# Column units of a hybrid decoder layer: all products with the high weights first, then all with the low weights

## The chip, the cores and the metric

The kernel runs on one core of one Trainium2 chip. The metric is the device time of one execution in microseconds, the median of several runs. Lower is better.

## The reference

One decoder layer on 256 tokens of width 1024 in float32. A modulated RMS norm gives `h`; one input projection gives ten blocks of 1024 columns; a causal attention with 8 heads and a short convolution run side by side; each has a SiLU gate and an output projection; the two are merged through sigmoid gates and go through a last projection and a residual, then a final RMS norm. With 256 tokens there is one attention block, so attention is plain causal attention with a relative bias.

```python
mod = jax.nn.silu(c) @ w_ada + b_ada
shift, scale, gate = jnp.split(mod, 3, axis=-1)
h = rmsnorm(x, norm_g) * (1 + scale[:, None, :]) + shift[:, None, :]
q, k, v, g_attn, cb, cc, cx, g_conv, m_attn, m_conv = jnp.split(h @ w_in, IN_OFFSETS, axis=-1)
attn = moba_attention(split_heads(q), split_heads(k), split_heads(v), rel_bias)
y_attn = (attn.transpose(0, 2, 1, 3).reshape(bsz, seq, ATTN_WIDTH) * jax.nn.silu(g_attn)) @ w_o_attn
y_conv = (short_conv(cb, cc, cx, conv_w) * jax.nn.silu(g_conv)) @ w_o_conv
merged = jax.nn.sigmoid(m_attn) * y_attn + jax.nn.sigmoid(m_conv) * y_conv
x = x + gate[:, None, :] * (merged @ w_out)
return rmsnorm(x, final_g)
```

## The kernel before

Precision is kept by splitting each float32 operand into a high part, held in the type `float32r`, and a low part, the rest. A product is then high times high, high times low and low times high, all summed in one PSUM bank.

The stages follow one another on PE (TensorE). After a start-up, the slab stage (L196 to L208) makes q and k for all heads, eight row tiles of the weights one after the other. Then come the V products (`rows_mm`, L349), and then 36 **column units** (`unit`, L332): four each of cc, cx, cb, gc, ga, ma, mc on the moving operand `H`, and four each of oa and oc, in turns, on `GA` and `GC`. The attention of the heads is put between the first units by a table of slots: scores (`pS`), transposes of the softmax (`pT`) and outputs (`pO`). At the end the output projection (`rows_mm` again, tiles `ao`) and the residual follow.

One unit makes 256 output columns as two halves (`t`) of 128. Its moving operand has, for each of the eight row tiles `k`, 512 columns: 256 of the high part, then 256 of the low part. For each `k` and half there are two products. The one with the high weights (L340) takes all 512 columns and fills a whole bank: the first 256 columns high times high, the others high times low. The one with the low weights (L341) takes the first 256 columns and adds to the bank's second half. `fold` (L324) then adds the two halves of the bank: ACT (ScalarE) copies the second half to SBUF (L326), DVE (VectorE) adds the first (L327). Below, the product of L340 is called wide, that of L341 narrow.

A unit's weights come as one DMA of 1 MB on SP's queue into one of five `raw` buffers. `split` (L67) makes the high part on ACT (L73) and the low part on DVE (L74), both for the whole unit at once, into one of three `hi` and three `lo` buffers. PSUM has eight banks, which all products share in turns (`bank`, L56).

The Tile framework finds the dependencies, puts in the semaphores, and plans at build time the order of the instructions on every engine, by priority in program order and by what its own model of durations finds ready. What is wrapped in `pin` keeps the order of the program; the products of a unit, its split and its fold are not pinned. Each engine then works through its own list in order.

Of the kernel before, what the change touches and what calls it, by code (L numbers as in the profile page):

```python
# [17 lines left out]
P = 128  # L18
D = 1024
S = 256  # L20
NH = 8
KT = D // P
# [21 lines left out]
def layer_kernel(ctx: ExitStack, tc, x, c, vec, wp_all, slab_all, onehot, final_g, out):  # L44
    nc = tc.nc
# [10 lines left out]
    def bank(name):  # L56
        return ps.tile([P, 512], F32, tag="acc", name=name, bufs=8)
# [4 lines left out]
    def load(key, name):  # L62
        t = raw_tile([P, 2048], name)
        nc.sync.dma_start(t, wp_all[UNIT[key]])
        return t

    def split(raw, shape, name, n=1, pin=lambda i: i):  # L67
        hi = wp.tile(shape, F32R, tag="hi", name=name + "h")
        lo = wp.tile(shape, F32R, tag="lo", name=name + "l")
        w = shape[1] // n  # L70
        for i in range(n):
            s = slice(i * w, (i + 1) * w)
            pin(nc.scalar.activation(hi[:, s], raw[:, s], AF.Copy))  # L73
            pin(nc.vector.tensor_sub(lo[:, s], raw[:, s], hi[:, s].bitcast(F32)))  # L74
        return hi, lo
# [248 lines left out]
    def fold(a, dst, name):  # L324
        low = tp.tile([P, S], F32, tag="low", name="low" + name, bufs=4)
        nc.scalar.activation(low, a[:, S:], AF.Copy)  # L326
        nc.vector.tensor_add(dst, a[:, 0:S], low)  # L327
# [4 lines left out]
    def unit(key, rhs, dst):  # L332
        name = f"{key[0]}{key[1]}"
        raw = load(key, "w" + name).rearrange("p (k n) -> p k n", k=KT)
        hi, lo = split(raw, [P, KT, 256], name)
        for t in range(2):
            a = bank(f"a{name}{t}")
            cols = slice(t * P, (t + 1) * P)
            for k in range(KT):
                nc.tensor.matmul(a, hi[:, k, cols], rhs[:, k, :], start=(k == 0), stop=False)  # L340
                nc.tensor.matmul(a[:, S:], lo[:, k, cols], rhs[:, k, 0:S], start=False, stop=(k == KT - 1))  # L341
            fold(a, dst[:, t, :], f"{name}{t}")
        return dst

    def put(src, dst, j, pin=lambda i: i):
# [12 lines left out]
    for n in range(2):  # L358
        av = [bank(f"av{n}{t}") for t in range(2)]
        for kh in range(2):  # L360
            if n == 0:
                hi, lo = v0[kh]
            else:
                raw = load(("v", n, kh), f"wv{n}{kh}").rearrange("p (k n) -> p k n", k=4)
                hi, lo = split(raw, [P, 4, 512], f"v{n}{kh}")
# [92 lines left out]
    for j in range(4):  # L458
        cc = unit(("cc", j), H, tmp("cc", f"cc{j}"))
        run_slot(n)  # L460
        n += 1
        cx = unit(("cx", j), H, tmp("cx", f"cx{j}"))
        run_slot(n)
        nc.vector.tensor_mul(cc, cc, cx)
        y = tmp("y", f"y{j}")
        for t in range(2):
            i = 2 * j + t
            nc.scalar.activation(y[:, t, :], cc[:, t, :], AF.Copy, scale=vT[:, 48 + i:49 + i])
            nc.vector.scalar_tensor_tensor(y[:, t, 1:], cc[:, t, 0:S - 1], vT[:, 40 + i:41 + i], y[:, t, 1:],
                                           op0=ALU.mult, op1=ALU.add)  # L470
            nc.vector.scalar_tensor_tensor(y[:, t, 2:], cc[:, t, 0:S - 2], vT[:, 32 + i:33 + i], y[:, t, 2:],
                                           op0=ALU.mult, op1=ALU.add)
        n += 1
        cb = unit(("cb", j), H, tmp("cx", f"cb{j}"))
        nc.vector.tensor_mul(YB[:, 2 * j:2 * j + 2, :], cb, y)
        run_slot(n)
        n += 1
# [66 lines left out]
    def residual(a, t, c0, w, slot, dst=None, scale=1.0, init=0.0):  # L544
        cols = slice(c0, c0 + w)
        g = slice(c0, min(c0 + w, D - S))
        if g.stop > c0:
            nc.vector.tensor_mul(TT[:, t, g], a[:, 0:g.stop - c0], gb[:, g])
            nc.vector.tensor_add(TT[:, t, g], TT[:, t, g], XR[:, t, g])  # L549
        if g.stop < c0 + w:  # L550
            r = slice(g.stop, c0 + w)
            nc.vector.tensor_add(TT[:, t, r], a[:, g.stop - c0:w], XR[:, t, r])
        if w == 512:
            nc.scalar.activation(SQ[:, t, 0:w], TT[:, t, cols], AF.Square, accum_out=s8[:, slot:slot + 1])  # L554
        else:
            nc.vector.tensor_tensor_reduce(SQ[:, t, 0:w], TT[:, t, cols], TT[:, t, cols], scale, init, ALU.mult,
                                           ALU.add, s8[:, slot:slot + 1] if dst is None else dst)
        return cols
# [20 lines left out]
    for n in range(2):  # L579
# [10 lines left out]
        else:  # L590
            tot = partial(0, 1)
            a = bank("ao2")
            for kh in range(2):
                rows_mm(a, M, 0, *w2[kh], 4 * kh, slice(0, 512), kh == 0, kh == 1)
            cols = residual(a, 0, 512, 512, 1)
# [3 lines left out]
            a = bank("ao3")[:, 0:S]  # L599
# [4 lines left out]
            a = bank("ao4")[:, 0:S]  # L604
# [70 lines left out]
```

## Time and profile before

| | us |
|---|---|
| median of 3 runs | 329.48 |
| lowest and highest of them | 328.32, 330.96 |
| span of the profiled execution, first to last instruction | 329.4 |
| PE busy in it | 321.4 |
| DVE busy | 247.3 |
| ACT busy | 189.0 |

The profile is of one execution and gives its span; the span stands 0.08 us below the median of the runs. The stages in its timeline: slab products from 15.6 to 65.8 us, V products to 87.6, the units with attention between them to 172.3, the other units to 300.9, the output projection and the tail to the end.

A row of the timeline gives the start and the duration in microseconds, the engine, the line, the operation, what it writes and reads, the shape, and in brackets the engine's idle time before it with what ended it. "x24" says that so many rows in sequence were merged. PEld is the weight load, which runs beside PE's products. A row of the grouped view gives busy time and mean nanoseconds of one instruction, then the idle time before.

### The profile page before, as it was taken

The page shows a single profiled execution, that of the slowest core. Times are in us where ns is not written, and L with a number is a line of the kernel's source. Part 1 is how long each engine was busy: PE and PEld are TensorE (multiplying, and loading weights), DVE is VectorE, ACT ScalarE, POOL GpSimd, SP SyncE. Part 2 cuts the span into 40 slices and gives each one's busy share as a digit, 9 for nine tenths or more (in the row PEclk, how much of TensorE's full clock was granted, in tenths as well). Part 3 has the DMA queues.
Part 4 walks back from the last instruction along what each step waited for, and adds up shares of the span by engine and source line. Part 5 has one row for each costly group of instructions (what it writes and reads, how often), then busy time and mean ns, then how long its engine had stood idle before and what let it go on. Part 6 is the DMA issues. An engine that isn't in the chain of part 4 may idle for free.

```text
span 329.4 us, 4903 instructions
## 1 busy us (share of the span) xinstructions
PE 321.4 (98%) x1870; PEld 281.9 (86%) x1870; DVE 247.3 (75%) x452; ACT 189.0 (57%) x305; POOL 5.6 (2%) x14
## 2 busy tenths in 40 slices
PE   8999999999999999999999999999999999999992
PEld 5689999988888888988888888888888888888892
DVE  2799993476388779697776998999946466787764
ACT  5654555364578676784768574856465635443430
POOL 3000000000000000000000000000000000000010
PEclk9999999999999999999999999999999999999998
DMA  6999999885645434543454469659875665400003
GB/s 240 406 409 403 410 412 352 309 303 214 247 150 200 171 129 141 211 160 127 137 206 169 142 217 373 225 193 370 346 294 205 228 218 202 182 0 2 0 0 127
DMA packets 14264, 72.75 MB, mean 221 GB/s; under 512 B 1523, under 2 KB 2819, under 8 KB 8098
## 3 DMA queue, kind: packets, MB, share of 16 engines
q1 hardware_dynamic: 12658, 70.40, 57.4%
q10 hardware_dynamic: 1488, 1.97, 1.9%
q8 instruction: 14, 0.23, 0.3%
q0 software_dynamic: 96, 0.09, 0.1%
q14 instruction: 8, 0.07, 0.1%
HBM read 71.39 MB, written 1.06 MB: 220 GB/s over the span
## 4 chain that ended last, share of the span: by engine, by line
PE 93%; DMA 2%; DVE 2%; ACT 1%; POOL 1%; SPq 0%; issue 0%; POOLq 0%; DVEq 0%; ACTq 0%
PE acc L205 15%; PE aoa L340 5%; PE acx L340 5%; PE aoc L340 5%; PE acb L340 5%; PE agc L340 5%; PE aga L340 4%; PE amc L340 4%; PE ama L340 4%; PE acc L340 4%; PE aoc L341 2%; PE aoa L341 2%; PE acx L341 2%; PE acc L341 2%; PE acb L341 2%; PE amc L341 2%
## 5 line engine op out<-in xcount | busy, mean ns | idle before, releaser
L205 PE MATMUL acc<-hf,slab 128*128 128x256 f32 x60 | 16.1, 418 | 0.0
L205 PEld LDWEIGHTS acc<-hf,slab 128*128 128x128 f32 x60 | 12.2, 213 | 3.0 <-ACT H L270 1.3
L155 DVE CUSTOM_DVE_ANT_0 ada<-ada,csb,vT 128x512 f32<-128x512 f32 (+1 forms) x18 | 12.3, 687 | 0.0
L155 DVE CUSTOM_DVE_ANT_0 ada<-ada,csb 128x512 f32<-128x512 f32 (+1 forms) x18 | 11.2, 626 | 0.5 <-DMA ada<-in_wp_dram 0.5
L407 DVE CUSTOM_DVE_ANT_0 L<-pS,BI 128x128 f32<-128x128 f32 x8 | 2.3, 292 | 12.2 <-PE pS L404 12.2
L306 DVE TENSOR_SCALAR QK<-acc 128x512 f32<-128x512 f32 x2 | 1.4, 686 | 9.1 <-PE acc L205 9.1
L572 POOL TENSOR_TENSOR rf<-ms,mhalf 128x1 f32<-128x1 f32 x2 | 1.7, 826 | 306.1 <-DVE ms L597 302.5
L554 ACT ACTIVATE SQ<-TT 128x512 f32<-128x512 f32 x3 | 1.9, 626 | 7.6 <-DVE TT L549 7.6
L304 ACT ACTIVATE QK<-acc 128x512 f32<-128x512 f32 x4 | 2.2, 601 | 7.0 <-PE acc L205 7.0
L377 DVE CUSTOM_DVE_ANT_0 gate<-gate,csb,vT 128x512 f32<-128x512 f32 x8 | 6.0, 744 | 0.3 <-DMA gate<-in_wp_dram 0.3
L139 PE MATMUL wt<-ones 128*128 128x128 f32 x20 | 5.0, 437 | 1.0 <-DVE parts L127 1.0
L340 PE MATMUL aoa<-GA,oa0h 128*128 128x512 f32 x16 | 5.8, 404 | 0.0
L340 PE MATMUL aoa<-GA,oa1h 128*128 128x512 f32 x16 | 5.7, 399 | 0.0
L340 PE MATMUL aoc<-GC,oc2h 128*128 128x512 f32 x16 | 5.7, 399 | 0.0
L340 PE MATMUL aoc<-GC,oc1h 128*128 128x512 f32 x16 | 5.7, 399 | 0.0
L340 PE MATMUL aoa<-GA,oa3h 128*128 128x512 f32 x16 | 5.7, 399 | 0.0
L340 PE MATMUL acx<-H,cx0h 128*128 128x512 f32 x16 | 5.7, 398 | 0.0
L340 PE MATMUL aoc<-GC,oc0h 128*128 128x512 f32 x16 | 5.7, 398 | 0.0
L340 PE MATMUL aoa<-GA,oa2h 128*128 128x512 f32 x16 | 5.7, 398 | 0.0
L340 PE MATMUL aoc<-GC,oc3h 128*128 128x512 f32 x16 | 5.7, 398 | 0.0
L340 PE MATMUL acc<-H,cc0h 128*128 128x512 f32 x16 | 5.7, 398 | 0.0
L340 PE MATMUL acb<-H,cb0h 128*128 128x512 f32 x16 | 5.7, 398 | 0.0
(460 smaller groups left out, 1221.9 us busy)
## 6 DMA issues: line engine op xcount, KB each, us to landing
slab<-in_slab_dram SPq DMA_DIRECT2D x16, 512.0 KB, 10.2
ada<-in_wp_dram SPq DMA_DIRECT2D x15, 512.0 KB, 10.2
wv<-in_wp_dram SPq DMA_DIRECT2D x4, 1024.0 KB, 10.6
wcc<-in_wp_dram SPq DMA_DIRECT2D x4, 1024.0 KB, 4.8
wcx<-in_wp_dram SPq DMA_DIRECT2D x4, 1024.0 KB, 4.8
wcb<-in_wp_dram SPq DMA_DIRECT2D x4, 1024.0 KB, 4.8
wgc<-in_wp_dram SPq DMA_DIRECT2D x4, 1024.0 KB, 4.8
wga<-in_wp_dram SPq DMA_DIRECT2D x4, 1024.0 KB, 4.9
```

Of the source, the lines that this page charges most:

```text
L139: pin(nc.tensor.matmul(wt[:, 0:P], ones, ones, start=True, stop=True))
L155: pin(nc.vector.tensor_tensor_reduce(src, src, csb[:, k:k + n], vT[:, i:i + 1] if s else 1.0, 0.0, ALU.mult, ALU.add, parts[:, i, s, k // ...
L205: pin(nc.tensor.matmul(acc[j // 2][:, (j % 2) * S:(j % 2 + 1) * S], w[i][:, j * P:(j + 1) * P], x, start=(i == 0 and j // 2 not in opened) ...
L304: pin(nc.scalar.activation(dst, src, AF.Copy, scale=scale))
L306: pin(nc.vector.tensor_scalar_mul(dst, src, scale))
L340: nc.tensor.matmul(a, hi[:, k, cols], rhs[:, k, :], start=(k == 0), stop=False)
L341: nc.tensor.matmul(a[:, S:], lo[:, k, cols], rhs[:, k, 0:S], start=False, stop=(k == KT - 1))
L377: nc.vector.tensor_tensor_reduce(src, src, csb[:, q * 512:(q + 1) * 512], 1.0, 0.0 if q else vT[:, 24 + b:25 + b], ALU.mult, ALU.add, gpar ...
L407: nc.vector.tensor_tensor_reduce(L[:, 0:P], pS[:, 0:P], BI[:, h, 0:P][:, ::-1], 1.0, -3.0e38, ALU.add, ALU.max, mx[:, 0:1])
L554: nc.scalar.activation(SQ[:, t, 0:w], TT[:, t, cols], AF.Square, accum_out=s8[:, slot:slot + 1])
L572: nc.gpsimd.tensor_tensor(r, ms, mhalf, op=ALU.pow)
```

## The change

The loop over the two halves is taken apart. Both banks are opened at the start of the unit. All 16 products with the high weights come first, half 0 and then half 1; then the eight narrow products of half 0 and its fold, then the eight of half 1 and its fold. The products themselves, their operands, the start and stop flags of each bank, the splits and the folds are as before.

```diff
         hi, lo = split(raw, [P, KT, 256], name)
+        accs = [bank(f"a{name}{t}") for t in range(2)]
         for t in range(2):
-            a = bank(f"a{name}{t}")
-            cols = slice(t * P, (t + 1) * P)
             for k in range(KT):
-                nc.tensor.matmul(a, hi[:, k, cols], rhs[:, k, :], start=(k == 0), stop=False)
-                nc.tensor.matmul(a[:, S:], lo[:, k, cols], rhs[:, k, 0:S], start=False, stop=(k == KT - 1))
-            fold(a, dst[:, t, :], f"{name}{t}")
+                nc.tensor.matmul(accs[t], hi[:, k, t * P:(t + 1) * P], rhs[:, k, :], start=(k == 0), stop=False)
+        for t in range(2):
+            for k in range(KT):
+                nc.tensor.matmul(accs[t][:, S:], lo[:, k, t * P:(t + 1) * P], rhs[:, k, 0:S], start=False,
+                                 stop=(k == KT - 1))
+            fold(accs[t], dst[:, t, :], f"{name}{t}")
         return dst
```

## The prediction

> **What bounds the kernel now.** I read the page first: engine shares, granted clock, chain of work that ended last.
>
> ```profile
> span 329.4 us, 4903 instructions
> PE 321.4 (98%) x1870; PEld 281.9 (86%) x1870; DVE 247.3 (75%) x452; ACT 189.0 (57%) x305; POOL 5.6 (2%) x14
> PEclk9999999999999999999999999999999999999998
> PE 93%; DMA 2%; DVE 2%; ACT 1%; POOL 1%; SPq 0%; issue 0%; POOLq 0%; DVEq 0%; ACTq 0%
> ```
>
> PE is in use for 98% of the span and holds 93% of the chain, at the full granted clock almost to the end. So the question is only how close together PE starts its products, and whether anything makes it wait. A busy PE does not show the first: a product's row overlaps the next one's. I therefore measured from start to start, with the timeline.
>
> ```profile
> 93.83 0.40 PE L340 MATMUL acx<-H,cx0h 128*128 128x512 f32 x1
> 99.48 0.49 PE L425 MATMUL pT<-ident,E 128*128 128x128 f32 x3
> 188.98 0.39 PE L340 MATMUL aga<-H,ga0h 128*128 128x512 f32 x1
> 211.16 0.39 PE L340 MATMUL ama<-H,ma0h 128*128 128x512 f32 x1
> 261.30 0.40 PE L340 MATMUL aoc<-GC,oc0h 128*128 128x512 f32 x1
> 300.87 0.40 PE L354 MATMUL ao<-o00h,M 128*128 128x512 f32 x1
> ```
>
> The reader sees two speeds for the same unit of 16 pairs. The four ga units take 22.18 us, 5.545 each, or 346.6 ns a pair. The seven units from oc0 to oc3 take 39.57 us, 5.653 each, or 353.3 ns a pair; cx0, amid attention, takes 5.65. I call these short and long units; a long one costs 0.107 us more. The grouped view by line says which are long, since a low-weight product's row is longer in them:
>
> ```profile
> L341 PE MATMUL aoc<-GC,oc2l 128*128 128x256 f32 x16 | 4.5, 281 | 0.0
> ...
> L341 PE MATMUL acb<-H,cb2l 128*128 128x256 f32 x16 | 4.5, 281 | 0.0
> ...
> L341 PE MATMUL acb<-H,cb1l 128*128 128x256 f32 x16 | 4.4, 277 | 0.0
> ```
>
> 15 of the 36 units have 281 ns (first and last shown): seven of the cc/cx/cb stage and all eight oa/oc. The other 21 have 280 or 277. Idle before these groups is 0.0: PE does not wait for weights or data.
>
> **The change part by part.** Nothing is added or removed: each unit keeps 16 wide products (512 columns, high weights), 16 narrow ones (256 columns, low weights), 32 weight loads, one DMA and two folds. Only the order moves.
>
> *Pace inside a run of equal products.* No unit of before has such runs, but two other stages do:
>
> ```profile
> 61.98 3.04 PE L205 MATMUL acc<-H,slab7h 128*128 128x256 f32 x24
> 64.86 1.12 PE L205 MATMUL acc<-H,slab7l 128*128 128x256 f32 x8
> 311.81 0.39 PE L354 MATMUL ao<-o10h,M 128*128 128x512 f32 x1
> 317.25 0.28 PE L354 MATMUL ao<-o10h,M 128*128 128x256 f32 x1
> 320.12 0.28 PE L354 MATMUL ao<-o10h,M 128*128 128x256 f32 x1
> ```
>
> 24 narrow products take 64.86 - 61.98 = 2.88 us, 120.0 ns each. 24 wide ones take 317.25 - 311.81 = 5.44 us, 226.7 ns each. A unit of runs is 16 x 226.7 + 16 x 120.0 = 5.547 us: the short unit to 2 ns, and 0.106 below the long one. So alternating is no waste of its own; only its longer beat is.
>
> *The switches.* Each unit will go once from wide to narrow and once, at the next unit, from narrow to wide. The first is seen at 317.25: the next 24 narrow products take 2.87 instead of 2.88 us, a gain of 0.01. The second is seen where the slab stage ends:
>
> ```profile
> 65.82 0.40 PE L354 MATMUL av<-v00h,H 128*128 128x512 f32 x1
> 71.29 0.39 PE L354 MATMUL av<-v01h,H 128*128 128x512 f32 x1
> ```
>
> These 24 wide products take 5.47 instead of 5.44 us, a loss of 0.03. Net 0.02 a unit. From oc3 into the output products (a long unit's alternation into a wide run) 24 took 5.50, a loss of 0.06, from these rows:
>
> ```profile
> 300.87 0.40 PE L354 MATMUL ao<-o00h,M 128*128 128x512 f32 x1
> 306.37 0.39 PE L354 MATMUL ao<-o01h,M 128*128 128x512 f32 x1
> ```
>
> I take 0.02, because a narrow run ahead of the wide one is what the new order has; the ends 0 and 0.06 stay for the range.
>
> *The sum on PE.* A new unit is 5.547 + 0.02 = 5.567 us. 15 long units gain 0.086 each, 1.29; 21 short ones lose 0.02 each, 0.42 to 0.46. Net -0.8 us. With no switch cost it is 15 x 0.106 = -1.6; with 0.06 it is -1.6 + 36 x 0.06 = +0.6.
>
> *The weight loads.* They lie beside products:
>
> ```profile
> L205 PEld LDWEIGHTS acc<-H,slab7h 128*128 128x128 f32 x32 | 4.0, 192 | 0.0
> ```
>
> A load's row is 192 ns, longer than a narrow product's interval. In the alternation every other interval is wide; in a narrow run none is. If loads could not overlap each other, a narrow run would go at 192 ns. The slab rows deny it: these very loads fed 24 products at 120 ns. The Trainium skill, "TensorE: Matmul & The Clock Gate", section "LDWEIGHTS (loading the stationary operand)", puts a load at columns over 1.2 GHz, 107 ns for 128, so an estimate by that page also leaves a narrow run at 120; the interval in the trace agrees.
>
> *The folds.* The first half's sums are complete after 16 wide and 8 narrow products, 4.59 us into the unit, instead of 2.77; the second half's at the end, as now. The two come 0.96 us apart, and one fold is
>
> ```profile
> 114.41 0.36 ACT L326 ACTIVATE lowcc<-acc 128x256 f32<-128x256 f32 x1
> 116.74 0.41 DVE L327 TENSOR_TENSOR cc<-acc,lowcc 128x256 f32<-128x256 f32 x1
> ```
>
> so the first fits before the second is ready. The second half's bank is opened 1.8 instead of 2.77 us into the unit; eight banks at two a unit return after four units outside attention, about two inside. I cost both at nothing; their cover is the time until the folded tile is used.
>
> *The splits.* Three high and three low buffers go round, and ACT's split waits for the high one:
>
> ```profile
> 183.51 1.92 ACT L73 ACTIVATE ga1h<-wga 128x2048 fp32r<-128x2048 f32 x1 [1.87 <-PE agc L340]
> 185.47 2.29 DVE L74 TENSOR_TENSOR ga1l<-wga,ga1h 128x2048 fp32r<-128x2048 f32 x1 [0.67 <-ACT ga1h L73]
> 194.52 0.39 PE L340 MATMUL aga<-H,ga1h 128*128 128x512 f32 x1
> ```
>
> The last wide product will end 16 x 0.12 = 1.9 us before the unit does, so ACT may start that much earlier; the low buffer comes free at the end, as now. Already the low part is ready at 187.76, 6.8 us ahead of use, and the low products start 3.6 us later still. This removes a wait of ACT that PE never feels: worth nothing, but it moves what is queued behind it on ACT and DVE. No DMA is added or moved past another; SP's loads keep their order and POOL has no part.
>
> *The tail.* M's last quarter and the last low weights are ready before PE needs them:
>
> ```profile
> 304.12 0.69 DVE L347 TENSOR_TENSOR M<-ya,M 128x512 fp32r<-128x512 f32 x1 [0.70 <-ACT M L346]
> 307.73 0.39 PE L354 MATMUL ao<-o01h,M 128*128 128x512 f32 x1
> 310.14 2.28 DVE L74 TENSOR_TENSOR o11l<-wo,o11h 128x2048 fp32r<-128x2048 f32 x1
> 314.53 0.39 PE L354 MATMUL ao<-o11h,M 128*128 128x512 f32 x1
> ```
>
> 2.9 and 2.1 us of room. The tail stays as it is.
>
> 329.4 - 0.8 = 328.6 us for this execution. The median of the three runs is 329.48, 0.08 above its span, so I say **328.7**.
>
> **The rivals.**
> *A: the long beat stays.* The two stages with long units may have it for a reason other than alternation, as operand addresses or work beside them. For it: all eight oa/oc units, whose moving operands are GA and GC, are long. Against it: short units use H, and so do seven long ones, at the same lines. Then there is no gain and the switches cost 36 x 0.02: 330.1 us.
>
> *B: the softmax chain becomes late, slower.* Here is the tightest place, one head:
>
> ```profile
> 112.58 1.92 ACT L73 ACTIVATE cc2h<-wcc 128x2048 fp32r<-128x2048 f32 x1 [1.24 <-PE acc L340]
> 113.86 0.29 DVE L407 CUSTOM_DVE_ANT_0 L<-pS,BI 128x128 f32<-128x128 f32 x1 [1.71 <-PE pS L404]
> 114.53 2.29 DVE L74 TENSOR_TENSOR cc2l<-wcc,cc2h 128x2048 fp32r<-128x2048 f32 x1
> 118.49 0.40 ACT L417 ACTIVATE E<-E,rr 128x128 f32<-128x128 f32 x1 [0.23 <-DVE rr L416]
> 119.31 0.49 PE L425 MATMUL pT<-ident,E 128*128 128x128 f32 x3
> ```
>
> E is done at 118.89, PE transposes it at 119.31: 0.42 us of room. With the high split earlier, the low split can run from 112.4, when its buffer comes free, while DVE idles 1.71 us for the scores; then it ends at 114.7 and the chain is shorter than now, as 2.29 us leave its middle. But if the planned order puts other work there (split and late first fold), a chain longer by more than 0.42 us stops PE, in program order. Where the whole 2.29 comes on top, it is 1.87 a head; over eight heads 15 us at most, 344 us; one extra fold of 0.36 + 0.41 leaves 0.35 a head, 2.8, on top of the forecast 331.5. I price it at 331.5 to 344, likelier near the lower end; it decides from 0.42 us of delay on.
>
> *C: the planned order is not what the text says*, with low products put back between high ones: 329.5.
>
> *D: loads bound the narrow run*, at 192 ns: 16 x (192 - 120) x 36 = 41 us, 370 us. Only an operand layout unlike the slab's could bring it.
>
> **How the numbers follow.** Forecast 0.66 (its own range 327.9 to 330.1, from the two ends of the switch cost), A 0.14, B 0.12, C 0.07, D 0.01. The three runs spread from 328.32 to 330.96, so 1% (3.3 us) is about what a measurement of this kernel can tell from no change. Below 326.2 no case leads, since PE has no wait to lose; I take 0.04 of the forecast for it. Above 332.8 lie D and B without a quarter for its mild end: 0.10. Within 1% remain 0.86. The range goes from the forecast's low end, 327.9, less 0.7 for the runs' spread, to just above B's lower edge, and leaves out 0.04 below and 0.10 above.
>
> **What would show it.** In the new timeline a unit without attention should take 5.55 to 5.58 us everywhere; wide starts 227 and narrow starts 120 ns apart; the first four or five wide ones a few ns slower. The oa/oc stage should come down from 39.57 to about 39.0 us for seven units, the four ga units up from 22.18 to 22.26. ACT's wait for L340 should shrink, DVE's idle time before the scores (1.71 us in the head shown) too.
>
> The prediction is wrong if PE shows idle time before pT, pS or pO, if narrow products stand wider than 120 ns apart, or if units still fall into two classes.

## The result, and the profile after

The changed kernel is slower, by about 1%: a median of 332.72 us (20 runs, 329.93 to 334.98) against 329.55 us for the kernel before (20 runs, 327.02 to 333.15), ratio 1.0106 with a 95% interval of 1.008 to 1.0133. Forecast were 328.7 us and a range of 327.2 to 331.8.

The page of the changed kernel, first its span and engine shares, then the head of the chain of work that ended last:

```profile
span 329.3 us, 4914 instructions
...
PE 319.0 (97%) x1870; PEld 282.1 (86%) x1870; DVE 248.1 (75%) x452; ACT 186.4 (57%) x305; POOL 5.6 (2%) x14
...
PE 87%; ACT 5%; DVE 4%; DMA 2%; issue 1%; POOL 1%; SPq 0%; POOLq 0%; DVEq 0%; ACTq 0%
```

The span alone would mislead: 329.3 us, as before. This execution took 331.13 us in all, and its start-up was 3.1 us shorter than in the profiled execution of before, which comes and goes whatever the order of the products (last section). What speaks is the chain: PE's share falls from 93 to 87%, and ACT's rises from 1 to 5%. So I read the run stage by stage, from the first product of one stage to that of the next. Here are the rows of the timeline that bound the stages, before and then after (start, duration; the start of the output products before, 300.87, stands in the prediction):

```profile
87.61 0.39 PE L340 MATMUL acc<-H,cc0h 128*128 128x512 f32 x1
...
177.88 0.39 PE L340 MATMUL agc<-H,gc2h 128*128 128x512 f32 x1
...
255.56 0.48 PE L340 MATMUL aoa<-GA,oa0h 128*128 128x512 f32 x1
```

```profile
84.51 0.84 PE L339 MATMUL acc<-H,cc0h 128*128 128x512 f32 x3
...
178.24 0.63 PE L339 MATMUL agc<-H,gc2h 128*128 128x512 f32 x2
...
256.19 0.48 PE L339 MATMUL aoa<-GA,oa0h 128*128 128x512 f32 x1
...
300.81 0.40 PE L356 MATMUL ao<-o00h,M 128*128 128x512 f32 x1
```

| us | attention stage: cc0 to gc2, 14 units | gc2 to oa0, 14 units | oa0 to output products, 8 units | sum |
|---|---|---|---|---|
| before | 90.27 | 77.68 | 45.30 | 213.26 |
| after | 93.73 | 77.96 | 44.62 | 216.30 |

The two stages without attention did what the prediction says: 14 short units lose 0.28, 0.02 each; eight long ones gain 0.68, 0.085 each. The loss is all in the attention stage: 3.46 us. Without waits its seven long and seven short units should have brought 7 x 0.02 - 7 x 0.086 = -0.46, so some 3.9 us of waits must stand there.

The view of waits (engine, operation, whom it waits for; us in total, times, the longest) and the grouped view by line name them:

```profile
PE pT L427 <- ACT E L419: 2.4, 5, 0.8
...
L427 PE MATMUL pT<-ident,E 128*128 128x128 f32 x24 | 4.2, 284 | 2.4 <-ACT E L419 2.4
```

In five of the eight heads PE waits, ahead of its transposes, for ACT's scaling of E; before, that line had 0.0. These 2.4 us count only the time after the modelled end of the last product. From start to start the five cost 0.92, 0.64 and three times 0.54 us; with 0.05 inside each of these transposes and 0.16 ahead of each of three late outputs `pO`, the intervals above the normal beat add up to 3.92 us. 3.92 - 0.46 = 3.46: nothing is left over. (The three late outputs use `ET`, a copy of the transposed E that ACT makes. In all three it comes right behind a split, in cc2 at 131.14 behind one that starts at 129.32.)

Why ACT is late is best seen in the head that the prediction showed. Its timeline after, ACT, then DVE, then PE:

```profile
115.25 0.49 ACT L416 ACTIVATE E<-L,mx 128x256 f32<-128x256 f32 x1
...
115.78 1.92 ACT L73 ACTIVATE cx2h<-wcx 128x2048 fp32r<-128x2048 f32 x1
117.60 0.38 ACT L419 ACTIVATE E<-E,rr 128x128 f32<-128x128 f32 x1
...
115.87 0.17 DVE L418 RECIPROCAL rr<-mx 128x2 f32<-128x2 f32 x1 [0.53 <-ACT E L416]
...
118.03 0.55 PE L427 MATMUL pT<-ident,E 128*128 128x128 f32 x3 [0.39 <-ACT E L419]
```

and of the kernel before the one row that stands behind the same scaling (118.49 there):

```profile
119.39 1.92 ACT L73 ACTIVATE cx2h<-wcx 128x2048 fp32r<-128x2048 f32 x1 [0.50 <-PE acx L340]
```

Before, the split of the next cx unit needed the unit's last wide product, so it came behind the scaling and cost nothing. Now the wide products end 1.9 us before the unit does, the split is free at once, and the planned order puts its 1.92 us between the exponentials and the scaling of E. The factor `rr` is there at 116.04; ACT starts the scaling at 117.60. PE starts its unit's last product at 117.37 and would by the narrow beat of 0.12 us have come to the transposes at 117.49; it starts them at 118.03.

Other work did the same in other heads. The first cx unit and the first cb unit after the change:

```profile
95.42 0.39 ACT L326 ACTIVATE lowcx<-acx 128x256 f32<-128x256 f32 x1 [0.30 <-PE acx L342]
96.37 0.38 ACT L326 ACTIVATE lowcx<-acx 128x256 f32<-128x256 f32 x1 [0.57 <-PE acx L342]
96.65 0.39 ACT L419 ACTIVATE E<-E,rr 128x128 f32<-128x128 f32 x1
...
97.10 0.55 PE L427 MATMUL pT<-ident,E 128*128 128x128 f32 x3 [0.76 <-ACT E L419]
...
102.59 1.90 ACT L73 ACTIVATE cb1h<-wcb 128x2048 fp32r<-128x2048 f32 x1
104.39 0.38 ACT L419 ACTIVATE E<-E,rr 128x128 f32<-128x128 f32 x1
...
104.83 0.55 PE L427 MATMUL pT<-ident,E 128*128 128x128 f32 x3 [0.47 <-ACT E L419]
```

In cx0 two folds stand ahead of the scaling, and the second waits until the unit's very last product: PE then waits for ACT, which had waited for PE. In cb0 it is a split again.

### The profile page after: what moved, and what is told of

Its sections match the earlier page's. It is cut to its first block, busy times and chain, and to the rows that moved or that the text cites. A ratio compares the mean times of both kernels' runs of the same rounds, so it can differ in the third digit from the quotient of the medians.

```text
span 329.3 us, 4914 instructions
## 1 busy us (share of the span) xinstructions
PE 319.0 (97%) x1870; PEld 282.1 (86%) x1870; DVE 248.1 (75%) x452; ACT 186.4 (57%) x305; POOL 5.6 (2%) x14
## 4 chain that ended last, share of the span: by engine, by line
PE 87%; ACT 5%; DVE 4%; DMA 2%; issue 1%; POOL 1%; SPq 0%; POOLq 0%; DVEq 0%; ACTq 0%
PE acc L205 15%; PE agc L339 4%; PE aga L339 4%; PE aoa L339 4%; PE aoc L339 4%; PE amc L339 4%; PE ama L339 4%; PE acc L339 4%; PE acb L339 3%; PE acx L339 3%; PE aoa L342 2%; PE ama L342 2%; PE aoc L342 2%; PE aga L342 2%; PE agc L342 2%; PE amc L342 2%
## 5 line engine op out<-in xcount | busy, mean ns | idle before, releaser
L505 ACT ACTIVATE SC<-mc 128x512 f32<-128x512 f32 x4 | 2.5, 632 | 10.3 <-DVE mc L327 7.5
L415 ACT ACTIVATE E<-L,mx 128x128 f32<-128x128 f32 x8 | 3.2, 396 | 8.5 <-DVE mx L413 8.5
L427 PE MATMUL pT<-ident,E 128*128 128x128 f32 x24 | 4.2, 284 | 2.4 <-ACT E L419 2.4
L505 ACT ACTIVATE SA<-ma 128x512 f32<-128x512 f32 x4 | 2.5, 634 | 5.8 <-DVE ma L327 5.7
L427 PEld LDWEIGHTS pT<-ident,E 128*128 128x128 f32 x24 | 2.6, 140 | 3.4 <-ACT E L419 3.4
L379 DVE CUSTOM_DVE_ANT_0 gate<-gate,csb 128x512 f32<-128x512 f32 x8 | 5.5, 684 | 0.0
L470 ACT ACTIVATE y<-cc,vT 128x256 f32<-128x256 f32 x8 | 3.9, 503 | 2.6 <-DVE cc L466 2.6
L139 PEld LDWEIGHTS wt<-ones 128*128 128x128 f32 x20 | 4.4, 328 | 1.1 <-DVE parts L127 1.0
L397 DVE TENSOR_TENSOR AX<-QK,AX 128x128 fp32r<-128x128 f32 (+1 forms) x16 | 5.1, 349 | 0.0
L326 ACT ACTIVATE lowoc<-aoc 128x256 f32<-128x256 f32 x8 | 2.7, 372 | 4.2 <-PE aoc L342 4.2
```

Source lines behind the costliest of these rows:

```text
L139: pin(nc.tensor.matmul(wt[:, 0:P], ones, ones, start=True, stop=True))
L379: nc.vector.tensor_tensor_reduce(src, src, csb[:, q * 512:(q + 1) * 512], 1.0, 0.0 if q else vT[:, 24 + b:25 + b], ALU.mult, ALU.add, gpar ...
L397: nc.vector.tensor_sub(lo, src, hi.bitcast(F32))
L415: nc.scalar.activation(E[:, 0:P], L[:, 0:P], AF.Exp, bias=mx[:, 2:3], accum_out=mx[:, 4:5])
L427: nc.tensor.transpose(pT[:, b * P:(b + 1) * P], E[:, b * P:(b + 1) * P], ident)
L505: nc.scalar.activation(dst[:, 2 * j:2 * j + 2, :], m, AF.Sigmoid)
```

## The experiments

My theory after this: the products are as fast as forecast, and the whole loss is **order on ACT and DVE**, work that became ready earlier and is planned ahead of the softmax's last step. The rival: the softmax **chain itself** is too long for the new order of products, whatever stands around it. A second rival: the loss belongs to the products in attention units. Below, three numbers in a row are the attention stage, the stage behind it and the oa/oc stage, as in the table above, each from one profiled execution; "cc0 to out" is that table's sum column.

**Where it is lost.** Two complementary kernels: the change in the cc, cx and cb units alone, and in all others alone.

```diff
+        if key[0] not in ("cc", "cx", "cb"):     # the other kernel: if key[0] in (...)
+            ...  the loop of before
+            return dst
```

> The new order in the 12 cc, cx and cb units alone; the other 24 alternate as before. Theory (the loss is PE waiting for the softmax, because the early free high buffer lets ScalarE's 1.9 us split run ahead of the softmax's last scaling): from the first cc0 to the first gc2 product 93.5 to 94 us as in the changed kernel (before: 90.27), from there to the first output product 123.0 as before; PE stands still 0.5 to 0.9 us ahead of the pT transposes of the cx units; the time is 3 to 4 us above before. Rival (the loss is spread over all units, or lies in the start-up): cc0 to gc2 within 1 us of 90.3 and the time within 1 us of before.

> The new order in the 24 gc, ga, ma, mc, oa and oc units alone; cc, cx and cb alternate as before. Theory: cc0 to gc2 about 90.3 us without a wait ahead of pT; gc2 to the first output product 122.5 (before 122.99); the time 0.3 to 0.6 us below before. Rival (loss spread over all units): two thirds of the loss stays, 2 us above before.

Attention units alone: stages 93.56, 77.68, 45.30; median 330.94 us, ratio 1.0077 (1.0049 to 1.0105). The others alone: stages 90.45, 77.96, 44.62; median 327.34 us, ratio 0.9967 (0.9931 to 1.0003), and no wait before pT. The two halves of the change simply add up, and the loss is bound to the attention units. The second kernel's run was repeated later:

> The change in all units but those of cc, cx and cb, a second time, beside the run with the softmax first. Theory: 90.4 us in the attention stage, 77.96 and 44.62 in the next two, time 0.2 to 0.5 us below before, and above the run with the softmax first by 0.4 to 0.7 us. Rival: the gain of 0.3 us in the first timing was chance, and the two come out alike.

It gave the same stages within 0.1 us (90.52, 77.96, 44.62) and 328.41 us, ratio 1.0013 (0.9981 to 1.0046). So the 0.3% of the first timing is not borne out; the stages give about 0.2 us.

**Taking away the early release.** The last wide product of a unit is put at its end, so that the high buffer comes free as late as before.

```diff
-                nc.tensor.matmul(accs[t], hi[:, k, ...], ...)     # 16 wide
+            for k in range(KT - t):                               # 15 wide, one kept back
+                high(t, k)
...
+            if t:
+                high(1, KT - 1, True)                             # behind all narrow products
```

> The new order in all units, but the last of the 16 products with the high weights is moved to the end of the unit, so that the high buffer comes free there, as before the change; the first fold stays late (4.36 us into the unit instead of 4.59). Theory (early high buffer): the waits ahead of pT go, cc0 to gc2 falls from 93.73 to 90 to 90.6 us, the time to 0.3 to 1 us below before. Rival (the late first fold crowds ScalarE and VectorE): the waits stay, cc0 to gc2 93 to 94 us.

Stages 91.50, 77.96, 44.62; median 330.2 us, ratio 1.0049 (1.0003 to 1.0094). All waits in the cx units are gone, but the stage stays above the 90 to 90.6 us that I expected: four waits of 0.345 us, one in each cb unit, with 0.05 inside the transposes behind each. ACT, DVE and PE in the second of these:

```profile
121.34 0.37 ACT L326 ACTIVATE lowcb<-acb 128x256 f32<-128x256 f32 x1
121.88 0.38 ACT L326 ACTIVATE lowcb<-acb 128x256 f32<-128x256 f32 x1 [0.17 <-PE acb L339]
122.16 0.39 ACT L427 ACTIVATE E<-E,rr 128x128 f32<-128x128 f32 x1
...
121.03 0.87 DVE L481 SCALAR_TENSOR_TENSOR y<-cc,vT,y 128x254 f32<-128x254 f32 x2
121.82 0.16 DVE L426 RECIPROCAL rr<-mx 128x2 f32<-128x2 f32 x1
...
122.61 0.55 PE L435 MATMUL pT<-ident,E 128*128 128x128 f32 x3 [0.18 <-ACT E L427]
```

The split is no longer in the way; now the folds are, and on DVE the convolution's `y` operations, which stand ahead of the reciprocal.

**Keeping the early release, binding the split alone.** An order constraint without a wait: on ACT, the split is issued behind the scaling of E of the head that it got ahead of.

```diff
-        hi, lo = split(raw, [P, KT, 256], name)
+        scaled = scales.get(len(traced) - 4)
+        traced.append(name)
+        with tc.issue_after(scaled.ins) if scaled is not None else nullcontext():
+            hi, lo = split(raw, [P, KT, 256], name)
```

> The changed kernel with one constraint on ScalarE's order alone: the high split that would run during a head's softmax is queued behind that head's last scaling of E. Nothing waits for more data than before. Theory (the split in front of the scaling is what holds pT): the waits of 0.54 us ahead of pT in cx1, cx2 and cx3 and of 0.64 us after cb0 go; the wait of 0.92 us in cx0, where the two folds of cx0 and not a split stand ahead of the scaling, stays. cc0 to gc2 falls from 93.73 to about 91.4 us. Rival (late first fold): the waits stay, 93 us or more.

Stages 92.00, 77.96, 44.62; median 329.38 us, ratio 1.0045 (1.0003 to 1.0087). The waits in cx1 to cx3 and behind cb0 are gone. In cx0, where folds and not a split were in the way, the wait is as long as in the changed kernel, 0.92 us from start to start:

```profile
98.34 0.55 PE L432 MATMUL pT<-ident,E 128*128 128x128 f32 x3 [0.76 <-ACT E L424]
```

The later cb units wait 0.24, 0.40 and 0.39 us, which I had not expected: there the convolution's `y` operations now stand ahead of the scaling. This separates the kinds of work: the split is one cause, and other work put ahead of the scaling, the folds in cx0, is another.

**Moving the scaling away from ACT.** If ACT's queue is what delays it, DVE may do it.

```diff
-        nc.scalar.activation(E[:, 0:P], E[:, 0:P], AF.Copy, scale=rr[:, 0:1])
+        nc.vector.tensor_scalar_mul(E[:, 0:P], E[:, 0:P], rr[:, 0:1])
```

> The changed kernel, with the scaling of the softmax's first part (128x128) moved from ScalarE to VectorE, so that the split on ScalarE no longer stands ahead of the transposes' last input. Theory: the waits ahead of pT in cx1 to cx3 (0.54 us each) and after cb0 (0.64) go, cc0 to gc2 at most 91.5 us, the time near before. Rival (late first fold, or VectorE itself too busy): the waits stay or grow, since VectorE gets 8 x 0.25 us more; cc0 to gc2 93.7 or more.

Stages 102.76, 77.96, 44.62; median 342.08 us, ratio 1.0409 (1.0354 to 1.0464). The cx waits are gone, but the whole is far slower than my theory's figure; it is the rival's, 93.7 us or more, that came true. The planned order is another one again, and three heads have a wait of 2.67 us. The first of them, ACT, DVE, PE, and the view of windows behind it (stretch, its length, busy time of PE, PEld, DVE, ACT and POOL, granted clock, DMA share, GB/s):

```profile
122.39 1.92 ACT L73 ACTIVATE cb2h<-wcb 128x2048 fp32r<-128x2048 f32 x1 [0.86 <-PE acb L339]
...
124.36 2.29 DVE L74 TENSOR_TENSOR cb2l<-wcb,cb2h 128x2048 fp32r<-128x2048 f32 x1 [1.38 <-ACT cb2h L73]
126.56 0.16 DVE L418 RECIPROCAL rr<-mx 128x2 f32<-128x2 f32 x1
...
127.36 0.33 PE L427 MATMUL pT<-ident,E 128*128 128x128 f32 x1 [2.51 <-DVE E L419]
...
124.50:127.40 2.90, 0.39 (x5) 0.20 (x4) 2.90 (x5) 2.47 (x10) 0.00 (x0) 1.00 0.02 6
128.50:131.80 3.30, 3.30 (x9) 2.61 (x8) 2.04 (x6) 0.34 (x2) 0.00 (x0) 0.51 0.71 300
```

The split stands ahead of the exponentials on ACT, and its low half ahead of the reciprocal on DVE: 1.92 + 2.29 us in the middle of the chain. It is the same mechanism, with both halves of the split in the way. Each of these waits also costs a second time: behind it the wide products stand 427 ns apart instead of 227 for some 3.4 us, and the granted clock reads 0.51. Seven products lose 0.2 us each that way, and their neighbours a little, so a wait of 2.67 us costs some 4.3 in all. Three of them are 13 us, the distance of this attention stage to one without waits (102.76 against 90.27 - 0.46).

**Other orders of the same products.** Runs by half (eight wide, eight narrow, then the other half), first plain, then with the last wide product at the end, and the latter only in the units with the long beat.

```diff
+        for t in range(2):
+            for k in range(KT - t):       # plain: range(KT)
+                high(t, k)
+            for k in range(KT):
+                low(t, k, ...)
+            if t:                         # plain: left out
+                high(1, KT - 1, True)
+            fold(accs[t], dst[:, t, :], f"{name}{t}")
```

> Runs of eight by half: high of half 0, low of half 0, high of half 1, low of half 1. The first fold comes at 2.77 us into the unit as before the change; the high buffer comes free 0.96 us ahead of the unit's end instead of 1.9. Theory: the folds no longer stand in front of the softmax in cx0; the split still may, where it is planned ahead of the scaling (in cb units by the planned order), so some waits after cb remain, 0 to 0.6 us each; cc0 to gc2 90.5 to 92.5 us. Two switches from narrow to wide in a unit instead of one: a unit without attention takes 5.59 instead of 5.567 us.

> Runs by half as in the former, and the last product with the high weights at the unit's end: the first fold is early and the high buffer comes free at the end, both as before the change. Theory: both causes of the waits are gone, no wait ahead of pT; cc0 to gc2 89.9 to 90.4 us, less than the 90.27 of before by what the runs gain over the longer beat, less the switches; the time 0.3 to 1 us below before. Rival (the runs themselves crowd the other engines): waits as in the changed kernel.

> The order of the former (runs by half, last high product at the end) in the cc, cx, cb, oa and oc units, where before had its longer beat; gc, ga, ma and mc alternate as before. Theory: cc0 to gc2 about 90.1, gc2 to oa0 77.7, oa0 to the first output product 44.7 us (before 45.30); in all 0.7 to 0.9 us below before. If the longer beat goes with what a unit is entered from, gc or ma units may show it now: then gc2 to oa0 is up to 16 x 0.1 us longer.

| us | attention stage | gc2 to oa0 | oa/oc | cc0 to out | median, ratio to before (interval) |
|---|---|---|---|---|---|
| runs by half | 92.94 | 78.24 | 44.78 | 215.95 | 332.39, 1.0105 (1.0035 to 1.0174) |
| and last wide at the end | 91.70 | 78.24 | 44.78 | 214.73 | 329.22, 1.004 (1.0 to 1.0081) |
| that in long units only | 91.62 | 77.68 | 44.79 | 214.09 | 331.07, 1.005 (1.0004 to 1.0095) |

Plain runs by half have waits of 0.92 us in three cb units, where a split stands ahead of the scaling: more than the 0.6 that I had allowed. With the release put back, my expectation that no wait stays failed: each cb unit keeps one of 0.35, with a fold and `y` operations ahead of the scaling, much as above; so the stage misses the 89.9 to 90.4 us, and the last kernel misses its 90.1. To put back one cause doesn't put back the planned order. Two by-products: twice the switches cost 0.28 us more over 14 units and 0.16 over eight, 0.02 a unit, the price that the prediction took from one place in the trace; and alternating units stay at the short beat (77.68) though the units before them changed.

**The softmax first.** Now the changed kernel with its products untouched, and only the order of ACT and DVE bound: the high splits, the folds and the `y` operations behind the scalings of E of their head.

```diff
+        with behind(scales, n - 4):
+            hi, lo = split(raw, [P, KT, 256], name)
...
+            with behind(scales, n - 1), behind(scales2, n - 1):
+                fold(accs[t], dst[:, t, :], f"{name}{t}")
...
+            with behind(scales, n), behind(scales2, n):
+                ...  the y operations
```

> The changed kernel; only the planned order of ACT and DVE is bound: in the attention stage the next split, the previous unit's folds and the convolution's y operations stand behind both scalings of E of their head. Theory (work put ahead of E's scaling is the whole loss): PE shows no wait before pT beyond 0.06 us anywhere, the attention stage from the first cc0 product to the first gc2 product takes 89.7 to 90.0 us (93.73 changed, 90.27 before), the stretch from cc0 to the output products 212.3 to 212.6 (216.30 and 213.26), and the time comes out 0.5 to 1.0 us below that of before. Rival (the softmax chain itself, its exponentials, reciprocals or the copies after pT, is too slow for this order of products): waits of 0.3 us or more before pT or pO stay, and the attention stage takes more than 91 us.

Stages 90.53, 77.96, 44.62; cc0 to out 213.11; median 328.12 us, ratio 1.0009 (0.9978 to 1.0041). That is short of the 89.7 to 90.0 us that I expected, but of 3.92 us of waits only some 0.8 are left, and 0.51 of these are one wait, in the third cb unit (ACT, then PE):

```profile
144.29 0.31 ACT L405 ACTIVATE AX<-V 128x128 fp32r<-128x128 f32 x1 [0.52 <-PE pO L450]
144.50 0.39 ACT L428 ACTIVATE E<-E,rr 128x128 f32<-128x128 f32 x1
...
144.94 0.55 PE L436 MATMUL pT<-ident,E 128*128 128x128 f32 x3 [0.35 <-ACT E L428]
```

A copy that I had not bound, that of a coming head's V columns, waits for PE's output products with the scaling behind it. The control, the same bounds with the products of before:

> The kernel before, with the same bounds on the planned order of ACT and DVE as the run with the softmax first. Theory: the kernel before has no wait of PE there, so nothing is to be gained: the attention stage stays at 90.2 to 90.4 us and the time within 0.3 us of before. Rival (the bound order alone is what speeds a kernel up, whatever the order of the products): the attention stage comes below 90.0 us here too.

Stages 90.27, 77.68, 45.30: to the hundredth the kernel before. The bounds alone bring nothing. Yet its median came out at 329.5 us, ratio 1.0043 (1.0007 to 1.0079): an interval that leaves out 1, though the stages are equal in the profiled executions. A difference of 0.4% in these times is therefore no proof of anything, and what follows goes by the stages.

**The rest of the waits.** First the copy of the V columns, which I put down to the wrong head:

```diff
+            slot = (h * 3) // 2 - 1 if c0 == 6 * P else None        # bound odd heads only
+            with behind(scales, slot), behind(scales2, slot):
+                nc.scalar.activation(hi, src, AF.Copy)
```

> The run with the softmax first, and the copy of the next odd head's V columns (which in the third cb unit stood ahead of E's scaling and waited for the output of an earlier head) behind E's scalings too. Theory: the last wait of over 0.11 us before pT, 0.51 us in that unit, goes, and no other comes; the attention stage takes 89.8 to 90.1 us (90.53 with the softmax first, 90.27 before), the stretch from cc0 to the output products 212.4 to 212.7 (213.26 before), the time 0.5 to 0.9 us below before. Rival (the wait moves to the next step that is nearly late): the attention stage stays at 90.4 us or more.

Stages 91.19, 77.96, 44.62; median 330.58 us, ratio 1.0048 (1.0003 to 1.0092). A miss: the copy in the way was the next even head's, and now it stood there in two cb units (0.51 each). With the copies of all heads bound, and then also the next cx unit's split behind the second head of a group:

```diff
-            slot = (h * 3) // 2 - 1 if c0 == 6 * P else None
+            slot = ((h - 1) * 3) // 2 if c0 == 6 * P else None
...
-        with behind(scales, n - 4):                                  # second kernel only
+        with behind(scales, n - (3 if key[0] == "cx" else 4)):
```

> The run with the softmax first, and the copy of every head's V columns behind the scalings of E of the head before it (in the last run only the odd heads' copies were bound, and the waits of 0.51 us came from the even heads'). Theory (the planned order is the whole loss): the 0.51 us waits before pT go, single waits of at most 0.15 us may stay where the second head of a group is scored late; attention stage 89.8 to 90.2 us, cc0 to output products 212.4 to 212.8 (213.26 before), time 0.4 to 0.9 us below before. Rival (the chain is too long for this order of products): waits of over 0.3 us stay in the cb units and the attention stage takes 90.4 us or more.

> As the run with every head's V copy bound, and the split of the next cx unit also behind the second head's scaling, so that its 2.29 us low split no longer stands ahead of that head's scores on DVE. Theory: no wait before pT over 0.06 us, attention stage 89.7 to 90.0 us, cc0 to output products 212.3 to 212.6, time 0.6 to 1.0 us below before. Rival (as above): waits of over 0.3 us stay, or the cx split is now late and PE waits for its weights at the next cx unit.

The first: stages 90.18, 77.96, 44.62, cc0 to out 212.75; median 329.09 us, ratio 1.0009 (0.9968 to 1.005). The waits of 0.51 us are gone, as expected. The second: stages 89.91, 77.96, 44.62, cc0 to out 212.48; median 327.18 us, ratio 0.9977 (0.9935 to 1.0019). Rows of the second: the four that bound its stages, and the head shown above, ACT and PE.

```profile
87.94 0.62 PE L347 MATMUL acc<-H,cc0h 128*128 128x512 f32 x2
...
177.85 0.40 PE L347 MATMUL agc<-H,gc2h 128*128 128x512 f32 x1
...
255.81 0.48 PE L347 MATMUL aoa<-GA,oa0h 128*128 128x512 f32 x1
...
300.42 0.40 PE L365 MATMUL ao<-o00h,M 128*128 128x512 f32 x1
...
117.47 0.40 ACT L430 ACTIVATE E<-E,rr 128x128 f32<-128x128 f32 x1 [1.62 <-DVE rr L429]
...
119.26 0.49 PE L438 MATMUL pT<-ident,E 128*128 128x128 f32 x3
```

E's scaling ends 1.4 us before PE comes to it, and PE's row has no wait. One wait of 0.19 us is left in the whole stage, in the last cb unit; the exception to what I had expected. The three stages are 213.26 - 212.48 = 0.78 us shorter than before: the gain of 0.8 that was forecast, with exactly the products that were forecast. The rival of a chain too long falls, and with it the one that puts the loss down to the products in the attention units, since these are the changed kernel's. Whether the kernel as a whole beats the one before by this 0.2% the times can't settle.

## Why the prediction was wrong

**The pace inside a run and the switches: right.** Four units after the change:

```profile
189.37 3.82 PE L339 MATMUL aga<-H,ga0h 128*128 128x512 f32 x16
...
211.64 1.09 PE L339 MATMUL ama<-H,ma0h 128*128 128x512 f32 x4
```

22.27 us, 5.567 each, as forecast (22.26 for the four); seven units from oc0 to oc3 take 38.97 us instead of 39.57 (forecast about 39.0). No unit is long any more, so rival A is out. Narrow products stand 120 ns apart, so rival D is out. With the waits taken away, the sum of -0.8 stands at -0.78.

**The folds: wrong in one unit.** "I cost both at nothing" failed in cx0, where two folds that wait for the unit's end stand ahead of E's scaling: 0.92 us. In the other four heads that made PE wait it was a split.

**The splits: the step that failed.** The text saw that ACT could split 1.9 us earlier, and said that this "removes a wait of ACT that PE never feels: worth nothing, but it moves what is queued behind it". It asked what the split *leaves*, the idle time, and not what it would then stand *in front of*. Worth nothing in the sum, the early splits cost some 2.9 of the 3.92 us of waits, by what stands ahead of each late scaling and each late `ET`; the folds in cx0 cost the rest. In the head shown, the split became ready just when ACT had nothing to do between the exponentials and the scaling, and there it went. The low split did leave the middle of the chain, as rival B's text expected, but it did not fit into DVE's idle time ahead of the scores. Rows after (DVE, DVE, PE) and before (PE, DVE):

```profile
111.03 2.29 DVE L74 TENSOR_TENSOR cc2l<-wcc,cc2h 128x2048 fp32r<-128x2048 f32 x1 [2.42 <-ACT cc2h L73]
113.90 0.28 DVE L409 CUSTOM_DVE_ANT_0 L<-pS,BI 128x128 f32<-128x128 f32 x1
...
111.81 0.28 PE L406 MATMUL pS<-AX 128*128 128x256 f32 x1
```

```profile
113.54 0.29 PE L404 MATMUL pS<-AX 128*128 128x256 f32 x1
...
118.29 0.17 DVE L416 RECIPROCAL rr<-mx 128x2 f32<-128x2 f32 x1
```

After the change DVE takes up the scores 2.09 us after the last score product starts, behind the low split and two folds; before, 0.32 us after it (113.86, in the prediction). From the start of that product to the end of the reciprocal the chain takes 4.23 us instead of 4.92, so 0.69 is gained. The same release gave more than that away on the other engine: with 1.92 us of split on top, the scaling ended half a microsecond too late.

**Rival B: it is what happened**, at a chance of 0.12. Its condition was right (more than 0.42 us of delay ahead of E's end, PE stopped in program order), and so was its sign of recognition, idle time before pT. Its price, 331.5 to 344 us, holds the 332.72; the measured sum is 3.92 us in five heads and three outputs, not 0.35 a head in eight. Its high end put the low split's 2.29 us into the chain; what came in, four times, was the high split's 1.92 us on ACT. What was missing was the ground for its chance. The planned order follows readiness, and a release that comes earlier by a known 1.9 us, for work of a known 1.92 us, on the engine that has to do the chain's last step, was no remote mishap. The high end of the range, 331.8, took in only its mild end.

**Rival C** is out: the products stand as the text has them, 16 wide starts and then 16 narrow.

## What to carry to other kernels

When a change frees a buffer earlier, write down which instruction that releases, how long it is, and what it will stand in front of on its engine: on an engine that works through its list in order, work that is off the critical path becomes part of it as soon as it is planned ahead of one step of the chain. Where a chain has less room (here 0.42 us) than the work around it is long (1.92 and 2.29 us), bind its order before changing anything that moves readiness; the gain of the new order of products was only there after that. And compare stages from first product to first product: spans and medians here moved by more than the 0.78 us that was to be gained, in the two spans read first because of the start-up.

## What the runs showed of the hardware that I had not expected

**An idle time of 2.5 us was followed by half the pace.** In the kernel with the scaling on DVE, 2.51 us of idle PE were followed, about a microsecond later, by some 3.4 us at half the granted clock (0.51 in the row above), three times; waits of 0.92 us in the traces of the other kernels were not. The Trainium skill, "TensorE: Matmul & The Clock Gate", section "Part 1: The HAM clock gate", gives the half rate as the state after at least one idle window of some 3.4 us. The trace agrees on the half, but here a shorter idle time was enough.

**The start-up has two paces.** The same first slab products, in the profiled executions of before and of after, and the windows row of before for that time (stretch, length, PE busy, granted clock, DMA share, GB/s):

```profile
16.65 2.34 PE L205 MATMUL acc<-hf,slab 128*128 128x256 f32 x5
...
15.63:18.00 2.37, 2.37 (x7) 1.00 1.03 413
```

```profile
16.67 2.10 PE L205 MATMUL acc<-hf,slab 128*128 128x256 f32 x9
```

Five products in the time of nine: before, eight of the first stand 427 ns apart, after, 216. The slab stage then takes 50.2 us instead of 48.3. It does so in two of the 16 traces: that of the kernel before and the last one above (50.24). The kernel before with the bound order, whose start-up is programmed the same, takes 48.3. The granted clock reads 1.00 in both kernels, so the records don't say that it is the clock. The start of the slab stage moves too, between 13.3 and 16.5 us. In the two traces of one and the same kernel (the change outside cc, cx and cb) the starts lie 1.83 us apart and the spans 1.75. Between the first two spans that I read, start (1.22 us) and pace (1.88 us) hid 3.1 us of the loss. Whether the two account for the whole spread of the runs that have no trace is not shown.

**What sets the long beat** of alternating products, 353.3 ns a pair in some units and 346.6 in others, stayed open: no run was made for it.
